# A hybrid transformer stack on one core: the recurrent blocks' short convolution summed in PSUM, and another order of pieces in three stages

## The chip, the cores and the metric

One core of one Trainium2 chip runs the whole program in a single launch. The metric is device time in microseconds of that launch, lower is better; the number given is a median of several runs. TensorE is called PE in the profile, its weight loads PEld, VectorE is DVE, ScalarE is ACT, GpSimd is POOL and SyncE is SP.

## The reference, cut to what matters

512 tokens of width 1024, float32. First come two layers of one kind (DEPTH = 2), then two layers with other mixers, cross-attention to a memory and gated feed-forwards. A layer of the first kind takes one normed input through three branches, whose outputs are joined and projected back:

```python
proj = h @ w_in[l]
...
y_nsa = nsa_attention(q, k_c, ..., gates, ...)
y_lru = rg_lru(u_lru, lru_conv_w[l], lru_conv_b[l], ...)
y_conv = conformer_conv(glu_a, glu_b, conv_dw_w[l], conv_dw_b[l], conv_ln_g[l], ...)
mixed = jnp.concatenate([y_nsa * silu(z_nsa), y_lru * silu(z_lru), y_conv * silu(z_conv)], -1)
x = x + mixed @ w_out[l]

def rg_lru(u, conv_w, conv_b, w_a, b_a, w_i, b_i, lam):
    xc = causal_dwconv(u, conv_w, conv_b)          # 4 taps for each of 512 channels
    ...                                            # gates from xc, then a scan over the tokens

def conformer_conv(ga, gb, dw_w, dw_b, ln_g, ln_b, w_pw2):
    u = causal_dwconv(ga * sigmoid(gb), dw_w, dw_b)  # 31 taps
    un = layer_norm(u) * ln_g + ln_b                 # over the channels
    return silu(un) @ w_pw2
```

The "latent-attention mixer" of the second kind of layer runs two attentions over the same normed input: C, whose queries, keys and values come from projections of rank 256 and 128, and D, over neighbourhoods of a 64-wide grid. Both have 8 heads of 64 and are projected back by one matrix.

## The kernel before

Activations lie feature-major: the residual stream is eight tiles X of 128 features x 512 tokens, and a branch of 512 channels is four such tiles. Every float32 product is done as three products of rounded parts (`mm3`, L407): hi x hi (L410), lo x hi (L411), hi x lo (L412), all summed in one PSUM bank. Weights stream from memory in chunks of 128x1024 (`weights`, L414): SP starts a DMA into wr, ACT rounds it to wh (L432), VectorE or POOL subtracts to get the rest wl (L365). `self.wp` is POOL's share of these subtractions in fourths, and the digits in the order strings of the first two layers set it.

A dense tile (`dense_tile`, L443) is one PSUM bank: for each of eight input tiles, three products of 128x512. PSUM has eight banks, tagged "msssstto" in the stages touched here: one m for dense tiles, four s for attention scores and other uses, two t for transposes and norm statistics, one o for attention outputs. While attention is under way (`self.quiet` is false) dense tiles have the single m bank only.

The order of the work is set by program order: a list scheduler gives instructions written earlier the higher priority, within what they depend on. The program is written as generators that are stepped by letters in strings:

- `block1` (L840), the two layers of the first kind, runs FIRST + SECOND (L837, L838). In FIRST, U steps `lru_front` (projection and short convolution, tile xc), G `conv_front` (conformer gate, evacuations gb and ga, long convolution, tile up into cy), K `compress` of the attention's keys and values, B and O `lru_back`, Z the gate tiles of the recurrence. In SECOND, T steps `conv_tail` (mean, subtraction, squares, rstd, silu, pointwise product and output), N and C the gate tiles z of attention and conformer (`silu_tiles`), A, Q, V and M the attention, X pairs of output tiles of the first attention half. "|" ties a piece to the last scores issued.
- `mixer_cd` (L1316) runs CD_FIRST and CD_SECOND (L298, L299): 0 to 3 project D's heads (`d_proj`, evacuation du), A to D are D's attention, i and r prepare C's latents (`c_in`, `c_prep`), 4 to 7 project C's heads (`c_proj`, copies cf and cvf), E to H are C's attention, o steps the output tiles of D.

An attention step (`attn`, L743 on) computes scores into an s bank (L743), takes the maximum on VectorE, the exponential p on ACT (L377), transposes p through a t bank (L798), copies it out as ptt (L805) and multiplies by V into the o bank (L813). `to_tok` transposes C's and D's values (L1313).

`ts` (L374) is a `tensor_scalar` on VectorE, `stt` (L368) a `scalar_tensor_tensor`: out = (a op0 scalar) op1 b. The conformer's norm in `conv_tail` sends channel sums through PE with a matrix of ones (`row_stats`, L514) and broadcasts them back with another product (`bcast`, L522).

Of the kernel before, what the change touches and what calls it, by code (L numbers as in the profile page):

```python
# [14 lines left out]
ALU = mybir.AluOpType  # L15
# [3 lines left out]
T = 512  # L19
# [267 lines left out]
class Net:  # L287
# [7 lines left out]
    WPRI = 1000000  # L295
    RPRI = 900000
    NW = {"w": 6}
    CD_FIRST = "0000iiiiA1rA111B2rB222C3C333D4D444D"  # L298
    CD_SECOND = "E5oE5o5F6oF6o6G7oG7o7HoH"  # L299
    CFG = {  # L300
        "b": dict(lay="msssstto", spare="msss", dense="ms", tok="ssss", stat="t", ahead=1, pv=-200, sc="vvvv", cp=0, low=-4000, wp=0),
        "a": dict(lay="msssstto", spare="msss", dense="ms", tok="ssss", stat="t", ahead=1, pv=-200, sc="vvvv", cp=0, low=-4000, wp=0),
# [45 lines left out]
    def par(self, name, i=0, n=1):  # L348
        o, w = self.pc.at[name]
        t = self.params0 if o + i + n <= KD else self.params  # L350
        return t[:, o + i:o + i + n]
# [483 lines left out]


    FIRST = "/UUG3cUp/GGUKGkKGgZZkZGZkkB/Q|AkOOkk/GkGONOAAQQkQAVM"  # L837
    SECOND = "0NMTMTTAAMATCAAACCCTNATQNQATTTTXTTT|AXAAAXA"  # L838

    def block1(self, l):  # L840
        xhl = self.norm(f"norm_g{l}")
# [9 lines left out]
        self.pins, self.last = "", {}  # L851
        for ch in self.FIRST + self.SECOND:
            if ch.isdigit():
# [93 lines left out]
    def lru_front(self, l, xhl):  # L947
        nc, par = self.nc, self.par
        w = self.weights(f"ul{l}")
        xcs = []  # L950
        for c in range(4):
            ps = self.dense_tile(w, xhl)
            up = self.sp.tile([P, 516], F32, name="lup", tag="lup", bufs=1)
            nc.gpsimd.memset(up[:, :3], 0.0)
            self.mul(up[:, 3:3 + T], ps, self.RB)
            xc = self.f("a", "xc")
            tap = lambda k: par(f"lcw{l}", c * 4 + k)
            self.ts(xc, up[:, 3:3 + T], tap(3), par(f"lru_conv_b{l}", c))
            for k in range(3):
                self.stt(xc, up[:, k:k + T], tap(k), xc, op1=ALU.add)  # L960
            xcs.append(xc)
            yield
        w = self.weights(f"lru{l}", raw=True)
        self.lru = []
        for c, xc in enumerate(xcs):
            if c % 2 == 0:
                m2, a_ = (self.pt(nm, [P, 2, T], F32) for nm in ("m2", "a_"))
                ibs = [self.f("p", "ib") for _ in range(2)]
                self.lru.append((m2, a_, ibs))
            e = c % 2  # L970
            col = slice(l * 4 + c, l * 4 + c + 1)
            tr, a2, ti = (self.f("a", nm) for nm in ("tr", "a2", "ti"))
            ps = self.ps("s")
            nc.tensor.matmul(ps, next(w), xc, start=True, stop=True)
            self.act(tr, ps, AF.Tanh, scale=0.5, bias=self.ba2[:, col])
            c4, nc4 = self.c4[:, col], self.nc4[:, col]
            self.act(a_[:, e, :], tr, AF.Exp, scale=nc4, bias=nc4)
            self.act(tr, tr, AF.Tanh, scale=c4, bias=c4)
            self.act(a2, a_[:, e, :], AF.Square)
            self.stt(m2[:, e, :], a2, 1.0, tr, op0=ALU.add)  # L980
            ps = self.ps("s")
            nc.tensor.matmul(ps, next(w), xc, start=True, stop=True)
            self.act(ti, ps, AF.Tanh, scale=0.5, bias=self.bi2[:, col])
            self.stt(ibs[e], ti, 1.0, xc, op0=ALU.add)
        for m2, _, _ in self.lru:
            self.act(m2, m2, AF.Sqrt, scale=0.25)
        yield
# [328 lines left out]
    def mixer_cd(self):  # L1316
# [84 lines left out]
        def c_attn(p, fq, fk, v):  # L1401
            box, take, row = self.outs()
            hs = []
            for g in range(2):
                rows = slice(64 * g, 64 * g + 64)
                hs.append((three(fq[g], fk[g]), lambda jj, rows=rows: v[:, jj, rows], row(rows), None))
            yield from self.attn(hs, full, True, True, 64, self.out_to(yc, box), pre=take)
# [7 lines left out]
        self.last = {}  # L1415
        for ch in self.CD_FIRST:
            if ch in "|/":
# [6 lines left out]
        for p in range(4):  # L1424
            steps["EFGH"[p]] = c_attn(p, *cqkv[p]) if cqkv[p] else None
        for ch in self.CD_SECOND:
            i = "EFGH".find(ch)
# [204 lines left out]
```

## Time and profile before

| | us |
|---|---|
| median of 3 runs | 2326.54 (2322.70 to 2330.18) |
| the profiled execution | 2326.87 |
| its span in the trace | 2324.8 |
| mean granted clock of TensorE | 0.972 of full |
| front of layer 0, 45 to 250 | 205 |
| second half of layer 0, 250 to 442 | 192 |
| front of layer 1, 442 to 675 | 233 |
| second half of layer 1, 675 to 866 | 191 |
| latent-attention mixer, 1566 to 1826 | 260 |

The stages not listed are the start (0 to 45), the first mixer of the second kind (866 to 1105), cross-attention and feed-forward (1105 to 1566) and, from 1826 on, memory projection, cross-attention, feed-forward and the end. A window of the trace is given in microseconds from the start of the span.

How to read the rows: a group of instructions shows line, engine, operation, output and inputs by the names of the program, tile size and count, then busy time in us and mean ns. A wait "PE ps_m L410 <- DVE z L368" is idle time of TensorE before its product of line 410 into bank m, ended by VectorE's instruction of line 368 that wrote z. In the timeline a bracket gives the idle time before an instruction and what ended it.

### The profile page before, as it was taken

To read this page: it belongs to the slowest core of one execution; us is meant where nothing else is said; L and a number is where in the kernel's file an instruction comes from. 1 tells how busy PE (TensorE), PEld (TensorE's weight loads), DVE (VectorE), ACT (ScalarE), POOL (GpSimd) and SP (SyncE) were. 2 spreads that over 40 slices of the span, in tenths; PEclk is the share of its full clock that TensorE was granted. 3 is DMA by queue.
4 is the path that set the end of the run, shared out by engine and by line. 5 is a ranking of instruction groups with operands and counts; after the bars stand their busy time and mean duration, and the time that the engine had idled before them with its cause. 6 is when DMAs were issued, how large, how long until landed. Compare 5 with 4: busy or idle time off the path is not lost. (4 is left out here: it accounts for less than half of the span.)

```text
span 2324.8 us, 29259 instructions
## 1 busy us (share of the span) xinstructions
PE 2189.0 (94%) x11068; PEld 1735.0 (75%) x11068; DVE 1488.6 (64%) x2552; ACT 960.0 (41%) x1821; POOL 339.2 (15%) x394
## 2 busy tenths in 40 slices
PE   8898999899998999898999999999998899999998
PEld 6677767676776668666878888878766688888887
DVE  8997676599886764786565544554766556554444
ACT  4422356425134653475453222232566454322223
POOL 4523100253320023001020000011000102000002
PEclk9999899999999999999999999999999999999999
DMA  4343211233331112311323333322312132332332
GB/s 142 92 136 88 71 42 32 64 96 113 105 105 46 36 54 75 92 47 46 118 81 93 98 98 93 100 91 78 97 53 70 46 109 73 100 97 93 98 93 91
DMA packets 61436, 194.73 MB, mean 84 GB/s; under 512 B 8432, under 2 KB 10480, under 8 KB 61296
## 3 DMA queue, kind: packets, MB, share of 16 engines
q1 hardware_dynamic: 52848, 179.75, 25.1%
q10 hardware_dynamic: 8448, 13.12, 2.1%
q8 instruction: 87, 1.43, 0.3%
q14 instruction: 53, 0.43, 0.1%
HBM read 182.61 MB, written 2.10 MB: 79 GB/s over the span
## 5 line engine op out<-in xcount | busy, mean ns | idle before, releaser
L432 ACT CAST wh<-wr 128x1024 fp32r<-128x1024 f32 (+2 forms) x312 | 323.4, 1037 | 697.1 <-DMA wr<-ws 581.3
L365 DVE TENSOR_TENSOR wl<-wr,wh 128x1024 fp32r<-128x1024 f32 (+1 forms) x265 | 328.7, 1241 | 358.0 <-PE ps_m L411 187.4
L410 PE MATMUL ps_m<-xh,wh 128*128 128x512 f32 x792 | 321.8, 406 | 28.0 <-DVE z L368 8.8
L412 PE MATMUL ps_m<-xh,wl 128*128 128x512 f32 x792 | 319.9, 404 | 4.7 <-POOL wl L365 4.4
L411 PE MATMUL ps_m<-xl,wh 128*128 128x512 f32 x792 | 317.8, 401 | 2.6 <-DVE xl L368 2.6
L412 PE MATMUL ps_s<-xh,wl 128*128 128x512 f32 x696 | 273.7, 393 | 6.5 <-DVE wl L365 6.5
L410 PE MATMUL ps_s<-xh,wh 128*128 128x512 f32 x696 | 274.5, 394 | 0.0
L411 PE MATMUL ps_s<-xl,wh 128*128 128x512 f32 x696 | 272.8, 392 | 0.0
L362 POOL TENSOR_TENSOR sq<-sq 128x512 f32<-128x512 f32 (+1 forms) x56 | 78.6, 1404 | 958.7 <-ACT sq L377 958.7
L410 PEld LDWEIGHTS ps_m<-xh,wh 128*128 128x128 f32 x792 | 153.5, 194 | 67.8 <-issue 15.2
L377 ACT ACTIVATE p<-ps_s,mn 128x512 f32<-128x512 f32 (+3 forms) x288 | 166.3, 582 | 69.5 <-PE ps_t L798 34.6
L412 PEld LDWEIGHTS ps_m<-xh,wl 128*128 128x128 f32 x792 | 153.4, 194 | 42.5 <-POOL wl L365 6.1
L411 PEld LDWEIGHTS ps_m<-xl,wh 128*128 128x128 f32 x792 | 153.4, 194 | 36.3 <-DVE xl L368 4.4
L368 DVE SCALAR_TENSOR_TENSOR ps_s<-up,params,ps_s 128x512 f32<-128x512 f32 x232 | 170.0, 750 | 2.6
L805 ACT COPY ptt<-ps_t 128x512 f32<-128x512 f32 (+3 forms) x288 | 132.3, 479 | 78.4 <-PE ps_t L798 76.5
L412 PEld LDWEIGHTS ps_s<-xh,wl 128*128 128x128 f32 x696 | 131.4, 189 | 37.0 <-DVE wl L365 9.1
L411 PEld LDWEIGHTS ps_s<-xl,wh 128*128 128x128 f32 x696 | 131.8, 189 | 28.0 <-issue 0.4
L410 PEld LDWEIGHTS ps_s<-xh,wh 128*128 128x128 f32 x696 | 131.6, 189 | 27.6 <-issue 0.4
L798 PE MATMUL ps_t<-consts,p 128*128 128x128 f32 x848 | 133.8, 281 | 7.9 <-ACT ptt L805 5.0
L365 POOL TENSOR_TENSOR wl<-wr,wh 128x1024 fp32r<-128x1024 f32 (+2 forms) x47 | 112.4, 2392 | 159.0 <-ACT wh L432 63.2
L798 PEld LDWEIGHTS ps_t<-consts,p 128*128 128x128 f32 x848 | 97.5, 141 | 48.3 <-ACT ptt L805 15.5
L362 DVE TENSOR_TENSOR X<-ps_m,X 128x512 f32<-128x512 f32 (+1 forms) x114 | 76.1, 668 | 58.4 <-PE ps_m L412 58.0
(510 smaller groups left out, 4140.2 us busy)
## 6 DMA issues: line engine op xcount, KB each, us to landing
wr<-ws SPq DMA_DIRECT2D x318, 512.0 KB, 3.6
strip<-strips ACTq DMA_DIRECT2D x8, 480.0 KB, 4.0
wr<-ws SPq DMA_DIRECT2D x8, 384.0 KB, 3.5
X<-x SPq DMA_DIRECT2D x8, 256.0 KB, 4.9
mem<-mem SPq DMA_DIRECT2D x8, 256.0 KB, 2.9
wr<-ws SPq DMA_DIRECT2D x7, 256.0 KB, 2.7
tab<-tables SPq DMA_DIRECT2D x6, 256.0 KB, 2.7
out_dram<-ox SPq DMA_DIRECT2D x8, 128.0 KB, 1.7
```

Source lines behind the costliest of these rows:

```text
L362: (eng or self.nc.vector).tensor_tensor(out=out, in0=a, in1=b, op=ALU.add)
L365: (eng or self.nc.vector).tensor_tensor(out=out, in0=a, in1=b, op=ALU.subtract)
L368: self.nc.vector.scalar_tensor_tensor(out=out, in0=a, scalar=s, in1=b, op0=op0, op1=op1)
L377: return self.nc.scalar.activation(out, in_, func, **k)
L410: mm(out, ah, bh, start=first, stop=False)
L411: mm(out, ah, bl, start=False, stop=False)
L412: return mm(out, al, bh, start=False, stop=last)
L432: nc.scalar.copy(wh[:, :n], wr[:, :n])
L798: nc.tensor.transpose(t[:, j * P:(j + 1) * P], p[:, j * P:(j + 1) * P], self.con("ident"))
L805: nc.scalar.copy(dst, src)
```

## The change

The short convolution of `lru_front` (four taps for each of four tiles in both layers) sums in a PSUM tile of tag t instead of in its SBUF output: the first tap and taps 0 and 1 write to `acc`, and tap 2 reads `acc` and writes xc. Beside that the strings SECOND, CD_FIRST and CD_SECOND change; FIRST does not. The number of instructions of each kind stays as it is.

```diff
--- before.py
+++ after.py
@@ -295,8 +295,8 @@
     WPRI = 1000000
     RPRI = 900000
     NW = {"w": 6}
-    CD_FIRST = "0000iiiiA1rA111B2rB222C3C333D4D444D"
-    CD_SECOND = "E5oE5o5F6oF6o6G7oG7o7HoH"
+    CD_FIRST = "000iiii01rAA111B2rB2223CC333D4D4D44"
+    CD_SECOND = "65E565EoooF6oGFG7o77HooH"
     CFG = {
         "b": dict(lay="msssstto", spare="msss", dense="ms", tok="ssss", stat="t", ahead=1, pv=-200, sc="vvvv", cp=0, low=-4000, wp=0),
         "a": dict(lay="msssstto", spare="msss", dense="ms", tok="ssss", stat="t", ahead=1, pv=-200, sc="vvvv", cp=0, low=-4000, wp=0),
@@ -835,7 +835,7 @@
 
 
     FIRST = "/UUG3cUp/GGUKGkKGgZZkZGZkkB/Q|AkOOkk/GkGONOAAQQkQAVM"
-    SECOND = "0NMTMTTAAMATCAAACCCTNATQNQATTTTXTTT|AXAAAXA"
+    SECOND = "0NMTMMTTAAATCAAACCCNTQTNQTATTTXTTT|AXAAAAAX"
 
     def block1(self, l):
         xhl = self.norm(f"norm_g{l}")
@@ -953,11 +953,11 @@
             up = self.sp.tile([P, 516], F32, name="lup", tag="lup", bufs=1)
             nc.gpsimd.memset(up[:, :3], 0.0)
             self.mul(up[:, 3:3 + T], ps, self.RB)
-            xc = self.f("a", "xc")
+            xc, acc = self.f("a", "xc"), self.ps("t")
             tap = lambda k: par(f"lcw{l}", c * 4 + k)
-            self.ts(xc, up[:, 3:3 + T], tap(3), par(f"lru_conv_b{l}", c))
+            self.ts(acc, up[:, 3:3 + T], tap(3), par(f"lru_conv_b{l}", c))
             for k in range(3):
-                self.stt(xc, up[:, k:k + T], tap(k), xc, op1=ALU.add)
+                self.stt(xc if k == 2 else acc, up[:, k:k + T], tap(k), acc, op1=ALU.add)
             xcs.append(xc)
             yield
         w = self.weights(f"lru{l}", raw=True)
```

How the strings move instructions is seen in the order of each engine. In each excerpt, a row is a run of like instructions. First VectorE in layer 0's second half, around the mean of the conformer's norm; z is the evacuation of a gate tile (L368), cy the convolution's output, sq its squares. Before:

```order
L368 SCALAR_TENSOR_TENSOR z<-ps_m,rb 128x512
L372 TENSOR_SCALAR mean<-ps_t 128x4
L365 TENSOR_TENSOR cy<-cy,ps_t 128x512 x4
L365 TENSOR_TENSOR wl<-wr,wh 128x1024
L368 SCALAR_TENSOR_TENSOR z<-ps_m,rb 128x512
L362 TENSOR_TENSOR sq<-sq 128x512 x2
```

With the change:

```order
L372 TENSOR_SCALAR mean<-ps_t 128x4
L365 TENSOR_TENSOR wl<-wr,wh 128x1024
L368 SCALAR_TENSOR_TENSOR z<-ps_m,rb 128x512
L365 TENSOR_TENSOR cy<-cy,ps_t 128x512 x4
L362 TENSOR_TENSOR sq<-sq 128x512 x2
L763 RECIPROCAL sc<-sm 128x4
L365 TENSOR_TENSOR wl<-wr,wh 128x1024
L359 TENSOR_TENSOR sc<-sc,gates 128x4
L368 SCALAR_TENSOR_TENSOR z<-ps_m,rb 128x512
```

A z that stood behind the mean and the four cy stands ahead of the cy now, and the next one behind them and the squares.

Second, TensorE at the boundary of two gate tiles in the same place, with the tiles' numbers, since the rows would read alike without them. Before (ps_m_2654 and ps_m_2690 are two tiles in the same bank):

```order
L410 MATMUL ps_m_2654<-xh_137,wh_2657 128x512
L411 MATMUL ps_m_2654<-xl_138,wh_2657 128x512
L412 MATMUL ps_m_2654<-xh_137,wl_2658 128x512
L410 MATMUL ps_m_2690<-xh_109,wh_2693 128x512
L411 MATMUL ps_m_2690<-xl_110,wh_2693 128x512
```

With the change, from the last product of one gate tile to the first of the next (without numbers):

```order
L412 MATMUL ps_m<-xh,wl 128x512
L798 MATMUL ps_t<-consts,p 128x128
L743 MATMUL ps_s<-kh,qh 128x256 x2
L743 MATMUL ps_s<-kh,ql 128x256 x2
L743 MATMUL ps_s<-kl,qh 128x256 x2
L798 MATMUL ps_t<-consts,p 128x128 x2
L514 MATMUL ps_t<-consts,sq 128x1 x8
L813 MATMUL ps_o<-ptt,v 64x256 x2
L813 MATMUL ps_o<-ptt,v 64x128 x2
L743 MATMUL ps_s<-kh,qh 128x384 x2
L743 MATMUL ps_s<-kh,ql 128x384 x2
L743 MATMUL ps_s<-kl,qh 128x384 x2
```

Attention's products and the sums of squares (L514) stand between the two tiles now.

Third, TensorE in the latent-attention mixer, at a value tile of C and its transposes (L1313), which read ScalarE's copy cvf of that tile. Before:

```order
L410 MATMUL ps_m<-ch,wh 128x512
L411 MATMUL ps_m<-cl,wh 128x512
L412 MATMUL ps_m<-ch,wl 128x512
L1313 MATMUL ps_t<-consts,cvf 128x128 x4
L798 MATMUL ps_t<-consts,p 128x128 x4
L410 MATMUL ps_m<-ch,wh 128x512
```

With the change:

```order
L410 MATMUL ps_m<-ch,wh 128x512
L411 MATMUL ps_m<-cl,wh 128x512
L412 MATMUL ps_m<-ch,wl 128x512
L743 MATMUL ps_s<-qkh 128x512 x2
L743 MATMUL ps_s<-qkh,qkl 128x512 x2
L743 MATMUL ps_s<-qkl,qkh 128x512 x2
L1313 MATMUL ps_t<-consts,cvf 128x128 x4
L798 MATMUL ps_t<-consts,p 128x128 x4
```

Six score products have come between the tile and its transposes. Before, two of the four value tiles have their transposes right behind them, now none.

## Rows read from the trace of the kernel before

**Rows 1.** The page, busy time, share of the span and instructions of each engine.

```profile
PE 2189.0 (94%) x11068; PEld 1735.0 (75%) x11068; DVE 1488.6 (64%) x2552; ACT 960.0 (41%) x1821; POOL 339.2 (15%) x394
```

**Rows 2.** Windows: length, busy PE, PEld, DVE, ACT, POOL; clock, DMA share, GB/s.

```profile
45.00:250.00 205.00, 185.46 (x883) 151.05 (x883) 184.77 (x254) 68.24 (x99) 78.74 (x50) 0.97 0.36 108
250.00:442.00 192.00, 179.76 (x1007) 131.57 (x1007) 129.09 (x351) 97.01 (x252) 6.91 (x20) 0.93 0.14 42
442.00:675.00 233.00, 215.61 (x998) 174.22 (x998) 197.28 (x262) 76.33 (x110) 92.37 (x64) 0.96 0.35 107
675.00:866.00 191.00, 178.02 (x1036) 130.61 (x1035) 131.41 (x355) 100.66 (x257) 8.43 (x15) 0.96 0.15 45
1566.00:1826.00 260.00, 244.54 (x1337) 186.86 (x1337) 150.47 (x283) 140.51 (x289) 18.72 (x51) 0.98 0.23 70
```

**Rows 3.** TensorE's waits in the span: total us, times, longest us.

```profile
PE ps_m L410 <- DVE z L368: 8.8, 7, 3.0
...
PE ps_m L410 <- DVE ga L368: 7.8, 2, 4.3
...
PE ps_s L743 <- ACT p L377: 4.7, 9, 1.6
...
PE ps_m L410 <- ACT cf L377: 4.4, 5, 1.3
PE ps_t L1313 <- ACT cvf L1395: 4.3, 2, 2.2
...
PE ps_t L1062 <- POOL t L362: 2.8, 2, 1.4
PE ps_m L410 <- DVE du L368: 2.7, 2, 2.1
...
PE ps_s L974 <- DVE gb L368: 1.8, 1, 1.8
```

**Rows 4.** Windows at half clock, first and last of five.

```profile
288.70:292.11 3.41, 3.41 (x10) 2.62 (x9) 0.69 (x1) 2.21 (x3) 0.00 (x0) 0.50 0.00 0
...
1793.98:1797.39 3.41, 3.41 (x11) 2.64 (x10) 0.00 (x0) 1.96 (x4) 0.00 (x0) 0.50 0.54 201
```

**Rows 5.** Timeline of TensorE at a boundary of gate tiles: start, length.

```profile
284.39 0.39 PE L411 MATMUL ps_m<-xl,wh 128*128 128x512 f32 x1
284.62 0.40 PE L412 MATMUL ps_m<-xh,wl 128*128 128x512 f32 x1
288.03 0.47 PE L410 MATMUL ps_m<-xh,wh 128*128 128x512 f32 x1 [3.01 <-DVE z L368]
```

**Rows 6.** VectorE's groups by form: busy us, mean ns, idle before.

```profile
L368 DVE SCALAR_TENSOR_TENSOR xc<-lup,params,xc 128x512 f32<-128x512 f32 x24 | 25.5, 1062 | 0.2
...
L374 DVE TENSOR_SCALAR xc<-lup,params 128x512 f32<-128x512 f32 x8 | 9.0, 1126 | 0.0
```

**Rows 7.** Tile xc (short convolution), its first taps.

```profile
L374 DVE TENSOR_SCALAR xc<-lup,params x8: 535/545/2610, 45.3 to 491.5; 128x512 f32<-128x512 f32 x8
```

**Rows 8.** Timelines of POOL and VectorE, layer 0's front.

```profile
55.94 2.79 POOL L365 TENSOR_TENSOR wl<-wr,wh 128x1024 fp32r<-128x1024 f32 x1 [2.77 <-PE ps_s L411]
...
57.05 2.23 DVE L368 SCALAR_TENSOR_TENSOR xc<-lup,params,xc 128x512 f32<-128x512 f32 x1
```

**Rows 9.** Tile up (long convolution): shortest/median/longest ns, first and last start.

```profile
L368 DVE SCALAR_TENSOR_TENSOR ps_s<-up,params,ps_s x232: 724/750/760, 50.8 to 648.7; 128x512 f32<-128x512 f32 x116
...
L374 DVE TENSOR_SCALAR ps_s<-up,params x8: 802/809/817, 49.4 to 614.3; 128x512 f32<-128x512 f32 x8
L368 DVE SCALAR_TENSOR_TENSOR cy<-up,params,ps_s x8: 735/743/753, 114.1 to 649.5; 128x512 f32<-128x512 f32 x8
```

**Rows 10.** Timeline of VectorE, layer 1's front.

```profile
544.11 0.69 DVE L368 SCALAR_TENSOR_TENSOR ib<-ti,xc 128x512 f32<-128x512 f32 x1 [2.38 <-ACT ti L377]
```

**Rows 11.** Timeline of VectorE, layer 0's second half, the subtractions.

```profile
283.66 2.48 DVE L365 TENSOR_TENSOR cy<-cy,ps_t 128x512 f32<-128x512 f32 x4 [5.31 <-PE ps_t L522]
```

**Rows 12.** Timeline of ScalarE in the same place, the last square.

```profile
291.06 0.63 ACT L377 ACTIVATE sq<-cy 128x512 f32<-128x512 f32 x1 [0.76 <-DVE sq L362]
```

## Prediction before the change was run

> **What bounds the kernel now.** I read the page's busy shares first [rows 1]: TensorE works 94% of the span, so a microsecond is won only where TensorE stands still or runs at half clock. A window for each stage [rows 2] gives that idle time as the stage less TensorE's busy time: 192.0 - 179.8 = 12.2 us in layer 0's second half, 13.0 in layer 1's, 15.5 in the latent-attention mixer (called CD below). In the two front halves it is 19.5 and 17.4, and there VectorE is just as full: 184.8 of 205 us (90%) and 197.3 of 233 (85%). The table of TensorE's waits [rows 3] names what ends them: in the second halves the evacuation of a gate tile (z), in CD the copies cf and cvf and the evacuation du, in the fronts POOL's t and VectorE's gb and ga. The windows at half clock [rows 4] come last: each of these starts just after such a wait (288.03 after 3.01 us [rows 5], then 288.70), lasts 3.41 us at a granted clock of 0.50, which is 1.2 of 2.4 GHz, and so loses half of it, 1.7 us of work. Three such windows lie on waits that the new order touches in the second halves, two in CD.
>
> The sum is made against the profiled execution, 2326.87 us, of which the span is 2324.8 and 2.07 lie around it. It is 0.33 above the median of the runs, 2326.54; nothing hangs on that. A measurement here tells about 0.3%, 7.0 us: below 2319.6 is faster, above 2333.5 slower.
>
> **Short convolution's sum in PSUM.** No instruction is added or removed. Before, 24 taps and 8 first taps take 25.5 + 9.0 = 34.5 us of VectorE [rows 6]. Their means, 1062 and 1126 ns, are far from the median of a first tap, 545 [rows 7]: some are stretched to 2.2 or 2.6 us, like the tap at 57.05 that runs while POOL computes a wl between 55.94 and 58.73 [rows 8]. The long convolution does the same arithmetic with its sum in PSUM already, in the same stretches, and its 232 taps never exceed 760 ns [rows 9]. I take its prices: 8 first taps x 0.809 + 16 x 0.750 + 8 x 0.743 = 24.4 us, a saving of 10.1 us of VectorE, some 5 a layer.
>
> How much reaches TensorE? It is in fronts where VectorE is 85 to 90% busy, and its lead shortens waits on it and on what it feeds: POOL's t (2.8 us in two waits) and gb (1.8) [rows 3] stand right behind these taps. I take these, 4.6 us. What is left of the lead is worth more only if it lasts until ga (7.8 us in two waits), and it meets places where VectorE itself waits for ScalarE, as 2.38 us for ti at 541.7 [rows 10]. So -4.6, bounded by -10.1 with three half-clock windows more (-15.2) on one side. On the other stands a first tap that alone changes: 0.809 - 0.545 is 0.26 us, eight times +2.1. The two ps_t banks cost nothing: between the four sums of a layer the order has only the norm's statistics on that tag.
>
> One rule speaks against this edit: the Trainium skill, VectorE: DVE Perf Modes, "Why PSUM operands drop a tier", says that any PSUM operand rules out the mode that needs both SBUF ports, and leaves fp32 at the plain rate. The trace agrees for the first tap (545 ns to SBUF, 809 to PSUM [rows 7, 9]); by that rule alone the term would be +2.1 and the sum 2306.6.
>
> **Second halves' order.** Before, two gate tiles follow each other in the one bank that dense tiles have during attention, with no product between: the second waits for z. At the worst place z is the fourth thing behind the mean of the conformer's norm, four cy subtractions of 2.48 us together [rows 11] and a wl, and TensorE stands 3.01 us [rows 5]. All z waits come to 8.8 us in seven [rows 3], nearly the same in both layers. In the new order score products, transposes and P.V products stand at that boundary; on VectorE one z goes ahead of the four cy, and the next comes behind them and the squares, but with those products to cover it. With three half-clock windows that gives -8.8 - 5.1 = -13.9.
>
> Something is late next. One bare boundary a layer is left; at the mean of the five shorter z waits, (8.8 - 2 x 3.01) / 5 = 0.56, that is +1.1. And TensorE now comes sooner to the sums of squares: between the mean's broadcast and them the order has 24 dense products at 0.23 us from start to start (284.39 to 284.62 [rows 5]), 5.5 us, and 12 narrower ones at half that at most, 6.9 in all, while the last square ended 291.69 - 283.66 = 8.0 us after the subtractions began [rows 11, 12]. That is 1.1 us a layer, +2.2. So -10.6, between -13.9 and, if the squares take it all, 0. A loss here is the slower rival below.
>
> **CD's order.** Of the waits, cf (4.4), cvf (4.3) and du (2.1 of 2.7 in one) are 10.8 us [rows 3], and two half-clock windows 3.4: -14.2. Behind du the new order has 12 score products, 12 x 0.23 = 2.8 us, more than the 2.1. Ahead of two of the cvf transposes, bare before, six score products stand now, 1.4 us against waits of up to 2.2: about 0.7 stays at each, +1.4. One bare boundary behind cf stays, up to +1.0. So -11.8. Bounds: -14.2, and 0 if the copies simply come as late as TensorE comes early.
>
> No DMA, weight chunk or byte is added; the engines that carry it are 0.14 to 0.36 busy in these stages [rows 2], so chunks asked for some microseconds sooner find room. No term.
>
> Sum: 2326.87 - 4.6 - 10.6 - 11.8 = 2299.9, say **2300**. Own range 2290 to 2312: the first end takes 10 us more, the short convolution's -10.1 and most of the add-backs; the other half of either order's term.
>
> **Rivals.**
> *The squares bound the second halves.* Everything that TensorE gains it loses at the sums of squares, since the chain from the mean over cy, squares, rstd to the dense products of the conformer is VectorE's and ScalarE's and no shorter than before. For it: 8.0 us against 6.9. Against: that is a difference of 1.1 us a layer, little beside a claim of 13.9 for both. 2326.87 - 4.6 - 11.8 = 2310.5.
>
> *Waits move.* VectorE's lead ends at waits for ScalarE [rows 10], and z, cf and cvf come late elsewhere; a few us at most are left: 2324. For it: TensorE's 94%. Against: the boundaries with nothing between are gone in the order itself.
>
> *Plain rate only.* The stretched taps stretch in PSUM too, or the time moves to their neighbours: 2306.6, as above. Against: 760 ns as longest in 232.
>
> *Slower: score banks.* A score product (L743) needs one of four ps_s banks, free only when ScalarE's exponential (p) has read it. Places where the order gives less than 1.6 us of TensorE work for that rise from 10 to 19 in the two layers, and fall from 13 to 8 in CD. If each of the 19 costs the longest such wait, 1.6 us, and every second one a half-clock window, 0.85 on average, that is 19 x 2.45 = 46.5 us: 2300 + 46.5 = 2346. It outweighs the gain of 27 from 11 places on, and is slower by more than 0.3% from 14. Against: today 23 such places have nine waits of 4.7 us together [rows 3], a fifth of a microsecond each.
>
> **How the numbers follow.** Forecast 0.52; squares bound 0.17; plain rate 0.03; more than forecast, under 2290 (the lead reaches ga, fewer half-clock windows; all upper bounds together 2283.6) 0.08; waits move 0.12, of which 0.11 within 0.3%; score banks 0.08. Faster is 0.52 + 0.17 + 0.03 + 0.08 + 0.01 = 0.81, same 0.11, slower 0.08. The range 2286 to 2322 leaves out the slower rival, half of the moved waits and half of the larger gains, 0.18.
>
> **What would show it.** Right: all taps of the short convolution at or under 0.82 us and some 5 us less VectorE in each front; z, cf, cvf and the long du wait gone from TensorE's table; the second half of layer 0 at a granted clock above 0.93 and some 5 us shorter; CD some 12 shorter. Wrong: sums of squares (L514) or their broadcast (L522) high among TensorE's waits, in place of z; waits of L743 for p grown from 4.7 to tens of us; VectorE's saving there, yet the fronts as long as before.

## The result and the profile after

| | before | with the change |
|---|---|---|
| median, us | 2328.21 (2322.70 to 2330.18, 4 runs) | 2285.48 (2283.62 to 2288.96, 4 runs) |
| ratio, 95% interval | | 0.9822 (0.9800 to 0.9844) |
| the profiled execution, us | 2326.87 | 2285.91 |

The change is 42.7 us faster by the medians, 41.0 by the two profiled executions. The forecast was 2300, 27 us faster. The median lies half a microsecond below the low end of the stated range, 2286 to 2322.

The page's busy times of the changed kernel answer to [rows 1]:

```profile
PE 2176.2 (95%) x11068; PEld 1733.4 (76%) x11068; DVE 1477.0 (65%) x2552; ACT 957.8 (42%) x1821; POOL 333.6 (15%) x394
```

The same five stages, cut at the same instructions of TensorE, with the columns of [rows 2]:

```profile
45.14:244.41 199.27, 184.83 (x883) 150.04 (x883) 178.92 (x254) 67.39 (x98) 76.88 (x50) 0.97 0.37 111
244.41:424.32 179.91, 174.15 (x1007) 129.97 (x1007) 129.21 (x351) 96.79 (x253) 6.64 (x20) 0.95 0.15 45
424.32:656.25 231.93, 216.57 (x998) 176.71 (x998) 192.75 (x261) 76.61 (x110) 89.57 (x64) 0.95 0.35 107
656.25:838.44 182.19, 176.01 (x1036) 131.94 (x1035) 132.78 (x355) 99.61 (x257) 8.61 (x15) 0.96 0.15 47
1537.74:1784.34 246.60, 240.08 (x1337) 184.37 (x1337) 150.57 (x283) 140.68 (x289) 18.48 (x51) 0.99 0.24 74
```

Set against [rows 2], the fronts lost 5.7 and 1.1 us, the second halves 12.1 and 8.8, CD 13.4: 41.1 in all, so the rest of the program gave nothing. Of it, 29.3 is TensorE's idle time (length less busy: 5.1, 2.0, 6.5, 6.8, 8.9 in the same order). The other 11.8 is shorter busy time, chiefly in the second halves (5.6 and 2.0) and in CD (4.5), where the granted clock went from 0.93 to 0.95, stayed at 0.96, and went from 0.98 to 0.99. How much of that the change has earned one profile can't say: h2 below, in the order of before, has 0.96 where the profile of before has 0.93.

TensorE's waits over the span, in the columns of [rows 3]:

```profile
PE ps_m L410 <- DVE X L362: 18.9, 10, 3.4
...
PE ps_m L410 <- DVE ga L368: 5.5, 2, 3.5
PE ps_s L743 <- ACT p L377: 4.7, 9, 1.6
...
PE ps_t L798 <- ACT ptt L805: 1.9, 7, 0.4
...
PE ps_m L410 <- DVE z L368: 1.5, 2, 0.7
PE ps_m L410 <- ACT cf L377: 1.4, 3, 0.5
PE ps_m L410 <- DVE du L368: 1.3, 3, 0.6
...
PE ps_t L1062 <- POOL t L362: 0.5, 1, 0.5
```

z fell from 8.8 to 1.5, cf from 4.4 to 1.4, POOL's t from 2.8 to 0.5, and the cvf row is gone. The score products' wait for p is where it was, 4.7. Two waits that the prediction did not name fell too. In the table of before, outside the rows that the prediction rested on, stand

```profile
PE ps_t L798 <- ACT ptt L805: 5.0, 10, 0.7
...
PE ps_m L411 <- DVE sl L365: 2.5, 2, 1.3
```

The first is 1.9 now, and sl (the conformer's silu, on its way into the pointwise product) no longer ends a wait in the table. On VectorE the short convolution's three forms are

```profile
L368 DVE SCALAR_TENSOR_TENSOR ps_t<-lup,params,ps_t x16: 739/752/761, 47.9 to 475.1; 128x512 f32<-128x512 f32 x16
L374 DVE TENSOR_SCALAR ps_t<-lup,params x8: 805/811/818, 45.4 to 472.5; 128x512 f32<-128x512 f32 x8
L368 DVE SCALAR_TENSOR_TENSOR xc<-lup,params,ps_t x8: 737/745/752, 50.5 to 477.1; 128x512 f32<-128x512 f32 x8
```

(shortest, median, longest ns). With the medians that is 16 x 0.752 + 8 x 0.811 + 8 x 0.745 = 24.5 us, where 34.5 stood; none is stretched.

### The profile page after: what moved, and what is told of

Same layout as the page of the kernel before. It is cut to its first block, busy times and chain, and to the rows that moved or that the text cites. A ratio compares the mean times of both kernels' runs of the same rounds, so it can differ in the third digit from the quotient of the medians.

```text
span 2283.9 us, 29303 instructions
## 1 busy us (share of the span) xinstructions
PE 2176.2 (95%) x11068; PEld 1733.4 (76%) x11068; DVE 1477.0 (65%) x2552; ACT 957.8 (42%) x1821; POOL 333.6 (15%) x394
## 5 line engine op out<-in xcount | busy, mean ns | idle before, releaser
L412 PE MATMUL ps_m<-xh,wl 128*128 128x512 f32 x792 | 314.4, 397 | 1.7 <-POOL lup L954 0.9
L368 DVE SCALAR_TENSOR_TENSOR ps_s<-up,params,ps_s 128x512 f32<-128x512 f32 x232 | 170.1, 750 | 2.5
```

Source lines behind the costliest of these rows:

```text
L368: self.nc.vector.scalar_tensor_tensor(out=out, in0=a, scalar=s, in1=b, op0=op0, op1=op1)
L412: return mm(out, al, bh, start=False, stop=last)
```

## Experiments

"The full change" is the changed kernel. An edit counts against the kernel before, as measured beside it on the same chip (2324.1 to 2326.3).

### One part at a time

Three runs make one part of the change alone, and a fourth undoes the short convolution's part.

**e1**, the sum in PSUM alone:

```diff
-            xc = self.f("a", "xc")
+            xc, acc = self.f("a", "xc"), self.ps("t")
...
-            self.ts(xc, up[:, 3:3 + T], tap(3), par(f"lru_conv_b{l}", c))
+            self.ts(acc, up[:, 3:3 + T], tap(3), par(f"lru_conv_b{l}", c))
...
-                self.stt(xc, up[:, k:k + T], tap(k), xc, op1=ALU.add)
+                self.stt(xc if k == 2 else acc, up[:, k:k + T], tap(k), acc, op1=ALU.add)
```

> The short convolution's sum in PSUM alone, both orders as before. Additive theory: the fronts give what they give in the full change (5.7 us in layer 0, 1.1 in layer 1), so 6 to 8 us faster than before, 2320 to 2322, VectorE's taps at 24.5 us instead of 34.5, second halves and the latent-attention mixer within 2 us of before. Rival, plain rate only: the stretch moves to neighbouring instructions and the time is within 2 us of before or 2 slower. Rival, interaction: the lead of the fronts is what the second halves use, and then 10 or more us come off already here, part of it in the second halves.

Measured: 2307.69 (2302.81 to 2313.80), ratio 0.9917 (0.9901 to 0.9933), 18.6 us faster. The profiled execution is the slowest of the six. Its fronts are 202.7 and 236.1 us long, for 205.0 and 233.0, which is 0.8 more together; but the second halves, whose lines the edit does not touch, lost idle time:

```profile
247.70:431.68 183.98, 174.10 (x1007) 127.98 (x1006) 129.43 (x351) 96.34 (x253) 7.33 (x20) 0.96 0.15 44
...
667.75:856.24 188.49, 177.85 (x1036) 131.76 (x1035) 132.74 (x356) 100.88 (x259) 9.04 (x16) 0.96 0.15 45
```

9.9 and 10.6 us idle, against 12.2 and 13.0. The order shows why: in layer 0's second half only 240 of TensorE's 1004 products stand at the place where they stood before. The front is redrawn too, though FIRST is the same: on VectorE 129 of 253 instructions of layer 0's front keep their place. The list scheduler places each instruction at a simulated time; where the simulated times change, the order there and behind is drawn anew. A drawn order is called a draw below.

**e2**, SECOND alone:

```diff
-    SECOND = "0NMTMTTAAMATCAAACCCTNATQNQATTTTXTTT|AXAAAXA"
+    SECOND = "0NMTMMTTAAATCAAACCCNTQTNQTATTTXTTT|AXAAAAAX"
```

> The string SECOND alone. Additive theory: the two second halves lose 12.1 + 8.8 us as in the full change, less what their half-clock windows vary by, so 17 to 21 us faster than before, 2307 to 2311; waits on z at most 1.5 us in all, waits on sl near zero. Rival, as forecast: 10.6 us, 2318, the rest of the second halves' 20.9 us belonging to the lead of the short convolution or to half-clock windows. Rival, interaction: under 10 us.

Measured: 2315.44 (2307.97 to 2323.73), ratio 0.9949 (0.9930 to 0.9968), 10.8 faster, the forecast's figure for this string. The profiled execution, the slowest of the six, keeps nearly the whole idle time of the second halves:

```profile
251.62:438.11 186.49, 174.47 (x1008) 128.07 (x1007) 128.44 (x352) 95.37 (x252) 7.33 (x20) 0.96 0.15 44
...
673.54:864.91 191.37, 179.47 (x1036) 131.89 (x1035) 131.23 (x356) 100.72 (x260) 9.11 (x16) 0.96 0.15 45
```

12.0 and 11.9 us, although the waits for z fell from 8.8 to 1.2 us over the span: the waits for ptt and p rose from 5.0 and 4.7 to 6.8 each. So the agreement of the total with the forecast isn't one of mechanisms. In this profile layer 0's second half is 5.5 us shorter, nearly all of it busy time at a granted clock of 0.96 for 0.93, and the two fronts are 4.1 us longer; where the other microseconds of the median went isn't settled by it. Over all runs the granted clock's median is 0.975, for 0.972 before, so part of the gain is clock.

**e3**, the two strings of CD alone:

```diff
-    CD_FIRST = "0000iiiiA1rA111B2rB222C3C333D4D444D"
-    CD_SECOND = "E5oE5o5F6oF6o6G7oG7o7HoH"
+    CD_FIRST = "000iiii01rAA111B2rB2223CC333D4D4D44"
+    CD_SECOND = "65E565EoooF6oGFG7o77HooH"
```

> The strings CD_FIRST and CD_SECOND alone. Nothing ahead of that stage changes, so 13 us in that stage and 11 to 14 us in the total, 2314 to 2317. If only the removed waits count and the half-clock windows there were chance, 9 to 10 us.

Measured: 2313.51 (2305.54 to 2322.85), ratio 0.9941 (0.9920 to 0.9963), 12.7 faster. The stage is a copy of the full change's, 247.0 us with 6.6 idle:

```profile
1563.97:1810.98 247.01, 240.43 (x1337) 184.54 (x1337) 150.35 (x283) 140.40 (x289) 18.48 (x51) 0.99 0.24 74
```

Here part and whole agree, since the order of this stage is the same in both.

**e4**, the full change with the sum in SBUF (the diff of e1, reversed):

> The full change with the short convolution's sum back in SBUF: both new orders, nothing else. Additive theory: 7 us slower than the full change, 2292, and the taps stretched again, 34 to 35 us. Plain-rate rival: as fast as the full change or 2 us faster. Interaction: 10 or more us slower than the full change, part of it in the second halves.

Measured: 2304.72 (2301.63 to 2307.80), ratio 0.9901 (0.9883 to 0.9918): 19 us slower than the full change. Up to CD its order on TensorE and VectorE is that of e2, instruction for instruction, and its second halves are idle for 12.2 and 12.0 us as there.

The three parts alone add up to 18.6 + 10.8 + 12.7 = 42.1 us, where the full change has 42.7. By their totals the parts look independent; the stages say otherwise, since e1 took its gain in large part in the second halves and e2 left the idle time there. For the short convolution two readings were left: the taps cost 19 us, or the order that the scheduler draws with them does.

### Taps and order held apart

The runs h1 to h4 fix the order. After the whole program is written down, each engine's instructions are chained in a given sequence by edges that order issue and wait for nothing; the sequence is that of another kernel, whose instructions correspond one to one:

```diff
+def hold(tc, nc):
...
+    traced = list(nc.cur_bb.bb.instructions)
...
+        for a, b in zip(seq, seq[1:]):
+            tc.add_manual_dep(traced[b], traced[a].name,
+                              mybir.DependencyInfo(mybir.DependencyClass.NoSync, mybir.DependencyReason.DATA),
+                              reason="held order")
...
         Net(tc, ctx, ap, pc).build(out, stages)
+        hold(tc, nc)
```

**h1**: program of e4 (sum in SBUF), order of the full change.

> The full change with the taps' sum back in SBUF, but every engine held to the full change's order, instruction by instruction (edges of issue order, no waits). Only the price of the taps and the waits in the fronts differ from the full change. Order theory: of the 19 us that lie between the full change and the run with the sum undone, the taps themselves are 5 to 8 us, in the fronts, and the rest is the second halves' order, which the scheduler also redraws when the taps change: 2291 to 2293 here, second halves idle as in the full change (5.8 and 6.2 us). Price theory: the stretched taps cost all 19: 2303 to 2305.

Measured: 2284.45 (2281.60 to 2288.50), ratio 0.9822 (0.9799 to 0.9846). The full change's time, with the taps in SBUF and stretched as before, if at fewer places:

```profile
L368 DVE SCALAR_TENSOR_TENSOR xc<-lup,params,xc 128x512 f32<-128x512 f32 x24 | 24.0, 1000 | 0.3
...
L374 DVE TENSOR_SCALAR xc<-lup,params 128x512 f32<-128x512 f32 x8 | 7.1, 885 | 0.0
```

31.1 us of taps. The price theory (2303 to 2305) falls; the order theory's 5 to 8 us for the taps was too much as well. The stages:

```profile
45.32:246.70 201.38, 185.55 (x883) 150.06 (x883) 182.79 (x254) 67.45 (x98) 80.40 (x50) 0.97 0.37 109
246.70:422.75 176.05, 170.50 (x1007) 126.59 (x1006) 128.38 (x351) 96.14 (x252) 6.57 (x19) 0.97 0.16 47
422.75:652.50 229.75, 212.95 (x998) 173.37 (x998) 196.10 (x264) 77.04 (x112) 90.98 (x64) 0.96 0.35 108
652.50:834.76 182.26, 175.94 (x1036) 131.72 (x1035) 131.99 (x355) 99.85 (x257) 8.53 (x15) 0.96 0.16 47
```

The fronts have 1.4 us more idle time each than the full change (15.8 and 16.8). In length they are equal, 431.1 us together for 431.2: the clock in layer 1's front is 0.96 for 0.95. Layer 0's second half is shorter than in the full change, at a granted clock of 0.97 for 0.95. That doesn't come from the taps: h4 below, in the same order with 25.6 us of taps, has 0.97 and the same 176.1 us there.

**h2**: program of e1 (sum in PSUM, old strings), order of before.

> The kernel before with the sum in PSUM and every engine held to the order of before. Order theory: 5 to 8 us faster than before, 2318 to 2321, all in the fronts, the second halves' idle time as before (12.2 and 13.0 us), where the same edit with a free order gave 18.6. Price theory: 2306 to 2309.

Measured: 2317.97 (2313.54 to 2324.62), ratio 0.9966 (0.9951 to 0.9981), 7.9 faster, as the order theory had it; the same instructions in the order of their own, e1, gave 18.6. The fronts' idle time is 16.2 and 13.3 for 19.5 and 17.4, that of the second halves 12.2 and 12.4, for 12.2 and 13.0. Of TensorE's waits, POOL's t fell from 2.8 to 1.3, the wait for gb (1.8) is gone and ga fell from 7.8 to 5.2, while z, at 8.4, is nearly where it was:

```profile
45.19:244.95 199.76, 183.59 (x883) 150.07 (x883) 179.05 (x254) 68.49 (x99) 76.07 (x50) 0.97 0.37 110
244.95:432.80 187.85, 175.68 (x1008) 128.83 (x1008) 129.07 (x351) 97.36 (x252) 7.13 (x20) 0.96 0.15 44
432.80:663.40 230.60, 217.35 (x998) 176.61 (x998) 189.87 (x261) 76.44 (x110) 91.55 (x64) 0.94 0.35 108
663.40:859.59 196.19, 183.83 (x1036) 134.92 (x1035) 131.90 (x354) 100.81 (x257) 8.54 (x15) 0.93 0.14 44
```

**h3**: the full change's program, order of e4.

> The full change's program (sum in PSUM, new strings), held to the order that the scheduler drew with the sum undone. Order theory: 5 to 8 us faster than the run with the sum undone, 2297 to 2300, second halves idle some 12 us each as there, so 12 to 14 slower than the full change with the very same instructions. Price theory: 2285 to 2287.

Measured: 2301.22 (2296.30 to 2306.06), ratio 0.9893 (0.9870 to 0.9915): 15.7 slower than the full change with the very same instructions, and 3.5 faster than e4, which is within the noise (e4's interval is 0.9883 to 0.9918). Its waits in layer 0's second half:

```profile
PE ps_m L410 <- DVE X L362: 4.0, 3, 2.7
PE ps_t L798 <- ACT ptt L805: 2.8, 3, 1.4
PE ps_s L412 <- DVE wl L365: 1.1, 1, 1.1
PE ps_t L798 <- DVE cy L365: 0.9, 1, 0.9
...
PE ps_m L410 <- DVE z L368: 0.4, 1, 0.4
...
```

those of the full change in the same stage:

```profile
PE ps_m L410 <- DVE X L362: 3.4, 2, 3.0
PE ps_m L410 <- DVE z L368: 0.7, 1, 0.7
PE ps_t L798 <- ACT ptt L805: 0.4, 1, 0.4
...
```

and those of before:

```profile
PE ps_m L410 <- DVE z L368: 4.2, 3, 3.0
PE ps_m L410 <- DVE X L362: 3.2, 1, 3.2
PE ps_t L798 <- ACT ptt L805: 1.8, 3, 0.6
PE ps_m L411 <- DVE sl L365: 1.3, 1, 1.3
...
```

Of z's 4.2 us, 0.4 and 0.7 are left, and of sl's 1.3 at most 0.2. In h3's order other waits stand in their place: ptt, wl and cy have 4.8 us there, where before ptt had 1.8 and wl 0.6, and X has 0.8 more. In the full change's order ptt has 0.4 and the other two are not in the table. "Waits move" was no wrong fear, then: it came true with the same strings, in the order that the scheduler drew without the PSUM sum.

**h4**: the full change in its own order, but the first tap writes SBUF and tap 0 reads it from there:

```diff
-            self.ts(acc, up[:, 3:3 + T], tap(3), par(f"lru_conv_b{l}", c))
+            self.ts(xc, up[:, 3:3 + T], tap(3), par(f"lru_conv_b{l}", c))
...
-                self.stt(xc if k == 2 else acc, up[:, k:k + T], tap(k), acc, op1=ALU.add)
+                self.stt(xc if k == 2 else acc, up[:, k:k + T], tap(k), acc if k else xc, op1=ALU.add)
```

> The full change, held to its order, with the first tap written to SBUF: tap 0 then reads two SBUF tiles and writes PSUM, taps 1 and 2 as in the full change. Theory that a tap is stretched when both of its inputs lie in SBUF, wherever it writes: tap 0 is as long as before on average (about 1.06 us), the first tap too (0.545 median, some at 2 or more), taps 1 and 2 at 0.75; some 4 to 6 us of VectorE come back and the time is 2 to 4 us above the full change. Rival, what counts is the output in SBUF: tap 0 stays at 0.75, only the first tap is stretched. Rival, plain rate: the first tap's 0.26 us is saved eight times and the time is 1 to 2 us below the full change.

Measured: 2284.64 (2281.83 to 2285.56), ratio 0.9818 (0.9795 to 0.9841): no difference from the full change that these runs can tell. The taps, in the columns shortest, median, longest:

```profile
L374 DVE TENSOR_SCALAR xc<-lup,params x8: 540/548/2121, 45.5 to 470.3; 128x512 f32<-128x512 f32 x8
L368 DVE SCALAR_TENSOR_TENSOR ps_t<-lup,params,xc x8: 745/760/1135, 47.7 to 471.4; 128x512 f32<-128x512 f32 x8
L368 DVE SCALAR_TENSOR_TENSOR ps_t<-lup,params,ps_t x8: 741/753/764, 49.0 to 472.7; 128x512 f32<-128x512 f32 x8
L368 DVE SCALAR_TENSOR_TENSOR xc<-lup,params,ps_t x8: 735/745/756, 50.3 to 474.7; 128x512 f32<-128x512 f32 x8
```

Tap 0, with both inputs in SBUF, is stretched to 1.14 us though it writes PSUM (1.78 at most in s1 below), so for it the output isn't what counts. For the first tap it is: with the same one input it is stretched to 2.1 into SBUF, and is at 0.82 at most into PSUM. The taps that read the sum from PSUM are never stretched. Tap 0's median is 760 all the same, since POOL meets it for long only once in this order; the first theory's mean of 1.06 us did not come. The groups' sum is 25.6 us, 1.1 more than in the full change, too little for the time to tell the theories apart.

### How much the order alone is worth

**s1** is h4's program with its order left to the scheduler.

> The full change with the first tap written to SBUF, as in the held run, but with the order left to the scheduler. The instructions are those of the held run, which took 2284.64 us. If the redrawn order is what most of the short convolution's gain comes from, this edit of one operand redraws it again and the time differs from the held run by more than a measurement's 5 us, to either side: 2279 or less, or 2290 to 2306 (the run with the sum undone had 2304.7). If the order is robust and the runs so far differ for another reason: 2282 to 2288, second halves idle near 6 us each.

Measured: 2300.22 (2296.88 to 2304.86), ratio 0.9898 (0.9881 to 0.9916). The same instructions, 15.6 us apart from h4 (the two were measured on different chips; by the ratios to before, 0.9898 and 0.9818, it is 18.6). The second halves are back near 12 us idle each:

```profile
249.25:435.94 186.69, 174.64 (x1007) 127.95 (x1006) 128.39 (x352) 95.27 (x252) 7.30 (x20) 0.96 0.15 44
...
667.02:859.92 192.90, 180.98 (x1036) 133.49 (x1035) 130.96 (x356) 100.31 (x259) 9.06 (x16) 0.95 0.15 44
```

This is hardly a third draw: in layer 0 its order on TensorE and VectorE is that of e4, instruction for instruction, and its time is near h3's. With the new strings two draws have been seen, one near 2285 and one near 2300 to 2305.

Six kernels in one table, the program's sum by row and the order by column, medians in us. The third column lacks the new strings, CD's among them:

| | order of the full change | order of e4 | order of before |
|---|---|---|---|
| sum in PSUM | 2285.5 (full change) | 2301.2 (h3) | 2318.0 (h2) |
| sum in SBUF | 2284.5 (h1) | 2304.7 (e4) | 2325.9 (before) |

Down a column the taps are worth -1.0, 3.5 and 7.9 us, of which the last alone is clear of the noise; along the rows the first two orders differ by 15.7 and 20.3. No run holds a kernel to its own order. That the holding itself costs nothing is taken from h1 and h4, which come out within 1.1 us of the full change in its free order.

**m1** tests whether places are what is paid for, by moving ten instructions of VectorE in the held order of the full change and nothing else. Each is an evacuation of bank m (or, once, a wl) for which TensorE waited while VectorE did other work first, as the last X of layer 0 behind an xl of 1.46 us and a wl of 1.21. In the sequence of VectorE, by place:

```
X  601 -> 599    X 1152 -> 1150    ga 791 -> 788    ga 238 -> 236    X 1756 -> 1754
X 1448 -> 1447   X 1451 -> 1450    X 2029 -> 2028   X 2032 -> 2031   wl 290 -> 288
```

> The full change held to its order, with ten instructions of VectorE moved ahead by one to three places and nothing else: nine evacuations of the one bank m (seven residual tiles X, two gates ga) and one wl, each of which stood behind other work of VectorE while TensorE waited for it 1.0 to 3.5 us. Order theory: what these stand behind is the price; the places alone are worth 2.3 + 2.6 + 2.2 + 1.1 + 2.5 + 1.3 + 0.9 + 1.2 + 1.0 + 1.2 = 16.3 us at most, half of it may come back as later wl, and half-clock windows behind the longer waits (three or four at 1.7) go too: 2262 to 2277. Rival: the waits come back at the next instruction on VectorE, whose work is no smaller: 2282 to 2288.

Measured: 2264.51 (2259.24 to 2271.57), ratio 0.9739 (0.9721 to 0.9756): 59.6 us faster than before and 21 faster than the full change (19 by the ratios to before, 0.9739 and 0.9822), the best version here. The rival, that the waits come back at the next instruction, falls. The profiled execution, the slowest of the five, is 14.3 us faster than the full change's, and TensorE's idle time over the span is 96.9 us for 107.7. Of its waits,

```profile
PE ps_m L410 <- DVE X L362: 10.4, 12, 2.0
...
PE ps_s L410 <- ACT wh L432: 5.4, 2, 3.1
...
PE ps_m L410 <- DVE ga L368: 1.9, 2, 1.1
```

X fell from 18.9 to 10.4 and ga from 5.5 to 1.9; a wait of 5.4 for wh, a weight chunk, is new.

## Why the prediction was right and where it was not

**What bounds the kernel.** Right: TensorE's idle places, and the half clock beside them. The idle time of the five stages fell by 29.3 us, and m1 gained by nothing but moving what TensorE waits for.

**The sum as a whole.** The direction was right, and every term came out larger: 6.8 us for 4.6, 20.9 for 10.6, 13.4 for 11.8. So 2285.5 is near the end where "all upper bounds together" had put 2283.6, and the prediction gave "more than forecast" a chance of 0.08, for another reason (the lead reaching ga, fewer half-clock windows). The step that failed is that each edit was taken to be worth what its own instructions change. An edit also redraws the order of stages that it does not touch, and the sum had no term for that. In the full change this came out as a gain; that it did is luck as far as the prediction goes, since nothing in it could tell one draw from the other.

**Short convolution.** On VectorE it came out within a tenth: 24.5 us where 24.4 was worked out. The fronts shortened by 6.8 us where 4.6 was taken, but this is no proof of the term: h1, in the same order with the taps in SBUF, has fronts just as short (431.1 us for 431.2 together). As a price of the edit alone, 7.9 us was measured in the order of before (h2), where the waits for t and gb went down as the term had them; in e4's order it was 3.5, not clear of the noise, and in that of the full change none that could be told. With its order left free the edit gave 18.6 (e1), of which 10.3 (2318.0 to 2307.7) is the redrawn order.

**The rule on PSUM operands.** The first tap went from 545 to 811 ns, as the prediction had weighed it; the "plain rate only" rival, in which the stretch stays or moves to neighbours, did not come: no tap of the sum was over 818 ns, and VectorE's busy time as a whole fell by 11.6 us (1488.6 to 1477.0). In the full change's own order, though, the edit gave no time that could be told (h1): there that rival's time stands, if not its reason.

**Second halves.** This is the term that was mis-sized: -10.6, with a bound of -13.9, where the two windows lost 20.9 us. The z waits went as said (8.8 to 1.5, where two bare boundaries of 0.56 were to stay). The 2.2 us to be given back at the sums of squares were not: no such wait is in the full change's second halves. And the bound counted only z, while over the span the waits for ptt and sl fell by 3.1 and 2.5 us more. With the bound drawn from the idle time of the stages, 25.2 us, instead of from one row of waits, 2286 would not have been the end of the range. Nor was the mechanism enough by itself. With the same string e2, e4, h3 and s1 have z waits of 1.2 us or less, and keep 11.5 to 12.2 us idle in each second half: there the time went to other waits. What fell from 12.2 and 13.0 to 5.8 and 6.2 is the idle time of one draw.

**CD.** Right: -11.8 forecast, 13.4 in the full change's window, 12.7 alone; cf, cvf and du as named, and the clock of the stage 0.99 for 0.98. The idle time fell by 8.9 us, where the waits less what was to stay made 8.4.

**The rivals.** The squares did not bound. The score banks did not either: the wait of L743 for p is 4.7 us in nine waits before and after, and 6.8 us in ten at most in the other runs (e2), far from the tens of us that were feared. "Moved waits" came true in e2, h3, e4 and s1, though only for the second halves.

**What stays open.** Which single place in the second halves' order decides isn't known; z alone does not. Why the taps' price can't be seen in the full change's order isn't known either: h1 has 2.8 us more idle time in the fronts than the full change, but only 1.0 more than h4, which ran on the same chip in the same order with 5.5 us less of taps, and took 0.2 us longer than h1. Part of e2's 10.8 us is not found in its one profile.

## What to carry to other kernels

Where a scheduler draws the order from simulated times, an edit is worth its own price plus a new draw, and the draw can be the greater part (15.7 us against 7.9 at most here): hold the order when the price of an instruction is asked, and look at the stages as well as the total, since here the totals of the single edits added up and the stages did not. Bound a stage's gain by its idle time and what it loses at half clock, not by the one wait that you mean to remove. Then look at what VectorE does just before each evacuation that TensorE waits for: moving ten of its 2552 instructions by one to three places gave 21 us.

## What the runs showed of the hardware

In these runs a tap on VectorE with its sum in PSUM keeps its pace beside POOL, where the same work in SBUF doesn't. In h4, POOL computes a wl, and the first tap, one input and output in SBUF, takes 2.12 us instead of 0.55:

```profile
451.55 2.40 POOL L365 TENSOR_TENSOR wl<-wr,wh 128x1024 fp32r<-128x1024 f32 x1 [3.42 <-PE ps_s L411]
```

```profile
452.16 2.12 DVE L374 TENSOR_SCALAR xc<-lup,params 128x512 f32<-128x512 f32 x1
```

In the full change the same two instructions meet again, with POOL at its own 2.40 us and the tap, now into PSUM, at 0.82:

```profile
454.11 2.40 POOL L365 TENSOR_TENSOR wl<-wr,wh 128x1024 fp32r<-128x1024 f32 x1 [3.68 <-PE ps_s L411]
```

```profile
455.06 0.82 DVE L374 TENSOR_SCALAR ps_t<-lup,params 128x512 f32<-128x512 f32 x1
```

The Trainium skill, SBUF — State Buffer, "Who interferes with whom", says that VectorE with two SBUF inputs, or in a mode that uses both ports, contends with a GpSimd instruction that reads SBUF, and with at most one such input outside that mode does not. The traces agree: in h4, tap 0 with two inputs takes 1.14 us at most beside POOL and 0.77 at most else, and the taps with the sum in PSUM 0.76 at most. The first tap into SBUF (2.12) agrees if it runs in such a mode; its 0.55 us alone, for 0.81 into PSUM, fits that, but no row names the mode. Not expected was how little it is worth: 6.6 us of VectorE between h1's taps (31.1) and the full change's (24.5), and no time that these runs can tell.
